# Two-layer trunk: the output projections begin with the rows that don't come from attention, keys and values stay on chip, the S5 output comes back in 8 loads, extra tiles accumulate over 4 row tiles

## The chip, the cores and the metric

The kernel runs on one core of a Trainium2 chip. The metric is device microseconds of one execution. The program before was run three times: 1918.76, 1931.55 and 1936.65 us, median 1931.55. A fourth number, of a profiled execution, belongs to the profile below.

## The reference, cut to what matters

Two layers over a sequence of 512 rows, width 2048, all in float32. Each layer modulates a normed input by a condition `c`, projects it, runs two mixers, gates each, and projects their concatenation back.

```python
def layer_attn_s5(x, c, ...):                       # layer 0
    h, gate = ada_modulate(x, c, norm_g, ada_w, ada_b)
    q, k, v, g_a, u, g_b = split_cols(h @ w_in, (1024, 256, 256, 1024, 1024, 1024))
    q, k = rope(rms_norm(q)), rope(rms_norm(k))
    o_a = gqa_block_attention(q, k, v) * jax.nn.silu(g_a)
    o_b = s5_mixer(u, ...) * jax.nn.silu(g_b)       # scan both ways, gelu, then y @ w_glu + b_glu, GLU
    return x + gate * (jnp.concatenate([o_a, o_b], axis=-1) @ w_out)

def layer_na_ssd(x, c, ...):                        # layer 1
    ...
    o_c = neighbourhood_attention(q, k, v, rpb) * jax.nn.silu(g_c)
    o_d = ssd_mixer(z, xbc, dt_raw, ...)
    return x + gate * (jnp.concatenate([o_c, o_d], axis=-1) @ w_out)
```

So rows 0 to 1023 of an output projection's input come from attention, rows 1024 to 2047 from S5 with its GLU (layer 0) or from SSD (layer 1). The S5 state passes work on 64 groups of 16 channels.

## The kernel before, in words

Every product of float32 matrices is made of three matmuls on values that are split into a high and a low part (`mm3`, L164 to L166, 512 columns each; `runit`, L228 to L230, 256 columns). Weights come in pieces of up to 128x1024 by `w_issue`, in the order of `plan0` and `plan1`, into two raw buffers; `w_prep` splits them (ACT copies the high part, L125, DVE subtracts for the low part, L126) into three buffers, and each unit takes the next (`w_take`). All DMAs are issued by one queue, SP's, in the order of the program.

The main line of the program is a list of units for TensorE: `tunit` (one output tile of 128 rows, 8 weight tiles of 128x128 to a weight piece), `runit` (the transposed kind, for q, k, v) and `out_units`. Beside it run generators ("streams"): after every few matmuls a unit calls `slot()`, which advances every stream by a step (by two while `sstep` is `SSLOT`). `finish(name)` calls slots until a stream ends. A scheduler orders the instructions of each engine by priorities; a slot's instructions have a higher one. PSUM has eight banks of 128x512: `m0` to `m3` and `b0` to `b3`. `mbank` turns through the first `nmain` of m0, m1, m2, m3. `tbank`, the bank for transposes, turns between `b2` and `m3` where `nmain` is under 4, and is always `b2` where it is 4.

Layer 0, in order:

- Input projection, k = 0 to 15: `ada_sum` (L966) sums the shift and scale of one row tile from two loaded buffers, `ada_cols` makes row tile k of `h`, and six banks accumulate 6 of the 8 tiles of `u`. Six further outputs (2 tiles of `u`, 4 gates of the S5 path) are the extra units: each takes a piece over 2 row tiles with 3 outputs, accumulates 6 matmuls in bank `b2`, and DVE adds the bank to `xacc` in SBUF (L1035; the first group is copied by ACT). They run at k = 2 to 17.
- The S5 stream (`s5_in`, `s5_scan`, `s5_kernels`, `s5_out`), which stores y to DRAM in 8 stores (L580). Beside it TensorE makes the gates `gb`, `ga` (`gate_evict`: L882 to L884, through `r2k`, a tile with a single buffer) and the k and v projections. `kv_evict` copies each bank by ACT to `r2k` (L1088), stores it to `kvd` (L1089), and both are loaded back (L1101) to G12 and G13.
- After the S5 stream: the rope tables (stream "tab"), `y_load` (L893: 64 loads of 16 partitions, 32 KB each, one for each group), and `ada_stream`, which reads 128x1024 pieces of the conditioning weights (L609), and reduces each with one DVE instruction (L623), one or two pieces to a slot by `ADAP`.
- Attention in four chunks (`gqa_stream`, 8 score steps to a chunk): scores, maximum (DVE, L828), exponent (ACT, L831), scaling (DVE, L837), four transposes into one bank (L813), a cast and a split (L125, L126), and the values. TensorE runs q projections and gates beside it, later the GLU units that read y (split on DVE at L1132).
- `finish("oa")`, the loads of the gated attention output, and then `out_units` from half 0, the attention's rows, with `nmain` 4.

In layer 1 the same `out_units` ran from half 1, after `finish("na")`.

Of the kernel before, what the change touches and what calls it, by code (L numbers as in the profile page):

```python
# [22 lines left out]
PRI_ADA = 3000  # L23
ADAP = "22221111"
NFIRST = 4
# [7 lines left out]
N1 = 6  # L33
AO = 6
S5K = (0, 0, 2, 2, 3, 3, 3, 4, 4, 4, 4, 4, 4, 3, 5, 5)
# [32 lines left out]
class Trunk:  # L68
# [111 lines left out]

    def out_units(self, rhs, evict, first, halves=False):

        bk = []
        for half in (first, 1 - first):
            for j in range(NFIRST):
                if half == first:
                    bk.append(self.mbank())
                wh, wl = self.w_take()
                for k8 in range(8):
                    c = slice(k8 * 128, k8 * 128 + 128)  # L190
                    self.mm3(bk[j], wh[:, c], wl[:, c], *rhs(half * 8 + k8), half == first and k8 == 0,
                             half != first and k8 == 7)
# [694 lines left out]
    def y_load(self, tag, ydram):  # L887

        ys = self.sl(tag, [128, 8, 8, 64])
        yv = ydram.rearrange("(t h) g c -> g h t c", h=16)  # L890
        for k in range(8):
            for g in range(8):
                self.nc.sync.dma_start(out=ys[16 * g:16 * g + 16, k], in_=yv[k * 8 + g])  # L893
            yield
        self.ys = lambda k: ys[:, k].rearrange("p t c -> p c t")
# [19 lines left out]
    def layer0(self):  # L915
        nc, A = self.nc, self.A
# [5 lines left out]
        def ada_load(k, qs=range(4)):  # L922
            if k < 16:
                if 0 in qs:
                    abuf[k] = big[k % 2].rearrange("p (q n) -> p q n", q=4)
                i = 2 * k - AO
# [92 lines left out]
        def extra(k):  # L1019

            wh, wl = self.w_take()
            g, half = k // 2 - 1, k % 2
            for i in range(3):
                e = 3 * half + i
                ps = self.bank("b2")
                for kk in range(2):
                    c = slice((3 * kk + i) * 128, (3 * kk + i) * 128 + 128)
                    self.mm3(ps, wh[:, c], wl[:, c], *self.h_rhs(2 * g + kk), kk == 0, kk == 1)
                if g == 0:
                    if e % 2 == 0:  # L1030
                        xacc.append(self.sl((G[16], G[17], G[0])[e // 2], [128, 2, 512]))
                    nc.scalar.copy(out=xacc[e // 2][:, e % 2], in_=ps)
                    continue
                t = xacc[e // 2][:, e % 2]
                nc.vector.tensor_tensor(out=t, in0=t, in1=ps, op=ALU.add)  # L1035
                if g == 7:
                    xev[e](t)

        for k in range(16):
# [10 lines left out]
            if k >= 2:  # L1050
                extra(k)
            for _ in range(S5K[k]):
# [13 lines left out]
        def s5_rest():  # L1066
            yield from self.s5_in([G[14], G[3], G[1], G[2], G[15], G[16], G[17]], st)
            a, b = self.s5_scan(st), self.s5_kernels(G[14:18])
            la = lb = True
            while la or lb:  # L1070
                la = la and next(a, "end") != "end"
                lb = lb and next(b, "end") != "end"
                yield
            yield from self.s5_out([G[14], G[15], G[3], G[16], G[10], G[17], G[11], G[0], G[2], G[1]], st, ydram)
        self.start("s5", s5_rest())
        self.sstep = SSLOT
        extra(17)
        for j in range(4, 8):
# [3 lines left out]
        kvd = self.scratch("kvd", [2, 128, 4, 256])  # L1082

        def kv_evict(i):
            def ev(bk):
                for j, b in enumerate(bk):
                    t = self.gt()
                    nc.scalar.copy(out=t, in_=b)  # L1088
                    nc.sync.dma_start(out=kvd[i][:, 2 * j:2 * j + 2].rearrange("p t c -> p (t c)"), in_=t)  # L1089
            return ev  # L1090
        for i in range(2):
            self.runit(self.h_lhs, (4, 4, 4, 4), 256, kv_evict(i))
        self.finish("s5")
        self.sstep = 1
        self.nmain = 4
        self.start("tab", self.qk_tables((G[8], G[10]), G[9]))
        self.start("yload", self.y_load("OLa", ydram))
        self.start("ada", self.ada_stream(range(3), G[15:18]))
        raw = [self.sl(t, [128, 4, 256]) for t in (G[12], G[13])]
        for i in range(2):  # L1100
            nc.sync.dma_start(out=raw[i], in_=kvd[i])  # L1101
        for j in GAK:
            self.tunit(self.h_rhs, 16, self.gate_evict(ga[j]))
        self.finish("tab")
        self.nmain = 3
        self.start("kT", self.gqa_k(raw[0], G))
        self.gqa_v(raw[1], G)
        aux = self.sl("OLb", [128, 4, 1024], F32R)
# [30 lines left out]
        for j in range(8):  # L1139
# [12 lines left out]
            for e in (ev_gate, ev_val):  # L1152
                self.tunit(lambda k: (yh(k), yl(k)), 8, e)
        self.finish("oa")
        self.nmain = 4
# [14 lines left out]
        def out_evict(j):  # L1170
# [22 lines left out]
            return ev  # L1193
        self.out_units(o_rhs, out_evict, 0, True)

# [454 lines left out]
    def layer1(self):  # L1650
# [125 lines left out]
        for c in range(4):  # L1776
            for nm, tg in (("k", G[14]), ("v", G[15]), ("q", G[16])):
# [22 lines left out]
        def out_evict(j):  # L1800
# [7 lines left out]
            return ev  # L1808
        self.out_units(o_rhs, out_evict, 1)

# [29 lines left out]
def host_layer0(I):  # L1840
# [17 lines left out]
    f["w0_u"] = w[:, 2560:3328].reshape(16, 128, 768)  # L1858
    f["w0_x"] = w[:, 3328:4096].reshape(8, 2, 128, 2, 384).transpose(0, 3, 2, 1, 4).reshape(8, 2, 128, 768)
# [3 lines left out]
    g = t_units(a("s5_w_glu")[0])  # L1863
    f["w0_glu"] = np.stack([g[8:], g[:8]], axis=1).reshape(16, 1, 128, 1024)
# [23 lines left out]
def plan0(A):  # L1888
    p = []
    for k in range(18):  # L1890
        if k < 16:
            p.append(A["w0_u"][k])
        if k >= 2:
            p.append(A["w0_x"][k // 2 - 1, k % 2])
# [6 lines left out]
    p += out_pieces(A["w0_out"], 0)  # L1901
    return p
# [74 lines left out]
```

## Time and profile before

| | before |
|---|---|
| median of 3 runs | 1931.55 us (1918.76 to 1936.65) |
| profiled execution | 1918.29 us, its span 1916.5 us |
| mean granted TensorE clock | 0.98 |
| PE / PEld / DVE / ACT busy in the span | 93% / 80% / 64% / 38% |
| DMA packets, bytes | 143243, 349.63 MB |

The profile gives the busy time of each engine over the span of one execution. PE is TensorE's matmul, PEld its weight load, DVE the VectorE, ACT the ScalarE, SP the engine that issues all DMAs. The rows of tenths cut the span into 40 slices of 47.9 us; a 9 is 90% or more, and in the clock's row 9 is the full granted clock. A wait names the instruction or DMA that ended the idle time of an engine. L12 is line 12 of the kernel.

### The profile page before, as it was taken

The page shows a single profiled execution, that of the slowest core. Times are in us where ns is not written, and L with a number is a line of the kernel's source. Part 1 is how long each engine was busy: PE and PEld are TensorE (multiplying, and loading weights), DVE is VectorE, ACT ScalarE, POOL GpSimd, SP SyncE. Part 2 cuts the span into 40 slices and gives each one's busy share as a digit, 9 for nine tenths or more (in the row PEclk, how much of TensorE's full clock was granted, in tenths as well). Part 3 has the DMA queues.
Part 4 walks back from the last instruction along what each step waited for, and adds up shares of the span by engine and source line. Part 5 has one row for each costly group of instructions (what it writes and reads, how often), then busy time and mean ns, then how long its engine had stood idle before and what let it go on. Part 6 is the DMA issues. An engine that isn't in the chain of part 4 may idle for free.

```text
span 1916.5 us, 28952 instructions
## 1 busy us (share of the span) xinstructions
PE 1791.1 (93%) x11176; PEld 1528.2 (80%) x11176; DVE 1230.5 (64%) x2357; ACT 731.5 (38%) x1360; POOL 38.7 (2%) x51
## 2 busy tenths in 40 slices
PE   5988799899949999979999999999999999999999
PEld 2755579689848987867888987887689999998887
DVE  7896667895558999963236567568986645544322
ACT  5432236325413544432224324435655434433211
POOL 2000000000000000001110000000000000000000
PEclk9999999999969999999999999999999999999999
DMA  8987452856789879745443573246743333342542
GB/s 316 355 308 263 114 138 76 267 162 207 235 271 318 297 240 307 242 138 165 140 140 102 175 265 102 88 123 204 217 144 128 104 105 98 101 141 76 191 143 88
DMA packets 143243, 349.63 MB, mean 182 GB/s; under 512 B 32544, under 2 KB 43712, under 8 KB 143104
## 3 DMA queue, kind: packets, MB, share of 16 engines
q1 hardware_dynamic: 143104, 347.77, 56.3%
q8 instruction: 88, 1.44, 0.3%
q14 instruction: 51, 0.42, 0.1%
HBM read 311.53 MB, written 34.61 MB: 181 GB/s over the span
## 4 chain that ended last, share of the span: by engine, by line
PE 56%; DVE 18%; DMA 17%; issue 4%; ACT 3%; SPq 1%; POOL 0%; DVEq 0%; ACTq 0%
PE m L164 11%; PE m L165 10%; PE m L166 10%; DMA G<-in_ada_r_dram 8%; PE m L228 5%; PE m L229 5%; PE m L230 5%; DVE wl L126 3%; DVE G L623 3%; DMA G<-s_ck 2%; PE b L164 2%; DVE w2k L477 2%; PE b L165 2%; DMA G<-csd 2%; PE b L166 1%
## 5 line engine op out<-in xcount | busy, mean ns | idle before, releaser
L125 ACT CAST wh<-w 128x1024 fp32r<-128x1024 f32 (+3 forms) x266 | 269.9, 1016 | 613.6 <-PE m L165 310.8
L126 DVE TENSOR_TENSOR wl<-w,wh 128x1024 fp32r<-128x1024 f32 (+3 forms) x266 | 314.9, 1184 | 276.5 <-ACT wh L125 267.9
L164 PE MATMUL m<-H,wh 128*128 128x512 f32 (+1 forms) x968 | 383.8, 400 | 4.9 <-ACT wh L125 3.5
L228 PE MATMUL m<-wh,H 128*128 128x256 f32 (+2 forms) x1232 | 355.4, 289 | 30.7 <-ACT r2k L1088 29.6
L165 PE MATMUL m<-H,wh 128*128 128x512 f32 (+1 forms) x968 | 382.3, 396 | 0.0
L166 PE MATMUL m<-H,wl 128*128 128x512 f32 (+1 forms) x968 | 378.2, 397 | 1.3 <-DVE wl L126 1.3
L230 PE MATMUL m<-wh,H 128*128 128x256 f32 (+2 forms) x1232 | 355.2, 290 | 0.0
L229 PE MATMUL m<-wl,H 128*128 128x256 f32 (+2 forms) x1232 | 354.3, 288 | 0.0
L228 PEld LDWEIGHTS m<-wh,H 128*128 128x128 f32 x1232 | 235.1, 191 | 35.7 <-ACT r2k L1088 30.2
L229 PEld LDWEIGHTS m<-wl,H 128*128 128x128 f32 x1232 | 235.1, 191 | 2.7 <-issue 1.0
L230 PEld LDWEIGHTS m<-wh,H 128*128 128x128 f32 x1232 | 234.5, 191 | 3.3 <-issue 1.7
L164 PEld LDWEIGHTS m<-H,wh 128*128 128x128 f32 x968 | 183.9, 190 | 51.3 <-ACT wh L125 7.3
L166 PEld LDWEIGHTS m<-H,wl 128*128 128x128 f32 x968 | 182.8, 189 | 43.6 <-issue 2.6
L165 PEld LDWEIGHTS m<-H,wh 128*128 128x128 f32 x968 | 183.3, 189 | 41.5 <-issue 3.7
L623 DVE SCALAR_TENSOR_TENSOR G<-G,cb 128x1024 f32<-128x1024 f32 x128 | 155.4, 1221 | 72.8 <-DMA G<-in_ada_r_dram 57.1
L164 PE MATMUL b<-H,wh 128*128 128x512 f32 x128 | 53.9, 430 | 11.8 <-DVE G L1035 11.6
L1388 ACT ACTIVATE G<-G,G 128x128 f32<-128x128 f32 x128 | 39.9, 390 | 49.8 <-DMA G<-csd 44.7
L1035 DVE TENSOR_TENSOR G<-G,b 128x512 f32<-128x512 f32 x42 | 28.6, 682 | 40.4 <-PE b L166 40.4
L164 PE MATMUL m<-OLb,wh 128*128 128x512 f32 (+1 forms) x132 | 50.1, 389 | 2.7 <-ACT OLb L125 2.7
L164 PE MATMUL m<-OLa,wh 128*128 128x512 f32 (+1 forms) x132 | 51.3, 391 | 0.2 <-ACT wh L125 0.2
L166 PE MATMUL m<-OLa,wl 128*128 128x512 f32 (+1 forms) x132 | 51.1, 387 | 0.0
L165 PE MATMUL b<-H,wh 128*128 128x512 f32 x128 | 51.1, 402 | 0.0
(395 smaller groups left out, 2754.7 us busy)
## 6 DMA issues: line engine op xcount, KB each, us to landing
G<-in_ada_r_dram SPq DMA_DIRECT2D x128, 512.0 KB
w<-in_w_kvq_dram SPq DMA_DIRECT2D x72, 512.0 KB
w<-in_w_out_dram SPq DMA_DIRECT2D x64, 512.0 KB
OLa<-in_ada_dram SPq DMA_DIRECT2D x32, 512.0 KB
OLb<-in_ada_dram SPq DMA_DIRECT2D x32, 512.0 KB
G<-s_ck SPq DMA_DIRECT2D x32, 512.0 KB
w<-in_w_x_dram SPq DMA_DIRECT2D x24, 512.0 KB
s_ck<-G SPq DMA_DIRECT2D x16, 512.0 KB
```

The source lines that it names most:

```text
L125: self.nc.scalar.copy(out=hi, in_=src)
L126: self.nc.vector.tensor_tensor(out=lo, in0=src, in1=hi.bitcast(F32), op=ALU.subtract)
L164: mm(out=out, lhsT=lh, rhs=rh, start=start, stop=False)
L165: mm(out=out, lhsT=lh, rhs=rl, start=False, stop=False)
L166: mm(out=out, lhsT=ll, rhs=rh, start=False, stop=stop)
L228: mm(out=o, lhsT=hi, rhs=wh[:, c], start=(k == 0 and i % per == 0), stop=False)
L229: mm(out=o, lhsT=hi, rhs=wl[:, c], start=False, stop=False)
L230: mm(out=o, lhsT=lo, rhs=wh[:, c], start=False, stop=last)
L477: tt(out=pt[..., g], in0=src, in1=self.s5_lt[..., g], op=ALU.mult)
L623: nc.vector.scalar_tensor_tensor(out=t, in0=t, scalar=1.0, in1=cb, op0=ALU.mult, op1=ALU.mult, accum_out=o)
L1035: nc.vector.tensor_tensor(out=t, in0=t, in1=ps, op=ALU.add)
L1388: nc.scalar.activation(out=r[:, d, c], in_=r[:, d, c], func=AF.Relu, scale=-1.0, bias=dv["hi"][:, c, 16 * d + h:16 * d + h + 1])
```

## The change

Five edits:

1. `out_units` always starts with half 1 for the first four output tiles (the S5/GLU or SSD rows), and calls `ready()` (the `finish` of the attention's output) before half 0. Layer 0's weight order follows. `nmain` is set to 4 before the rest of the attention's steps.
2. `raw_evict` copies k and v to G12 and G13, and the store and reload of `kvd` go. The rope tables move into the S5 stream, between `s5_in` and the scan. The k and v preparation starts before the gate units `GAK`, which now turn through 3 banks.
3. `y_load` is 8 loads of 128 partitions (256 KB); the host orders the rows of the GLU weights to match.
4. Extra units take 4 row tiles with 2 outputs: 12 units of 24 matmuls (12 per bank), at k = 4 to 18 but not where k % 4 is 3, instead of 16 units of 18.
5. `ADAP` from 22221111 to 22111111: the group 1 of the ada stream does one piece to a slot instead of two.

```diff
-ADAP = "22221111"
+ADAP = "22111111"
...
-    def out_units(self, rhs, evict, first, halves=False):
+    def out_units(self, rhs, evict, ready, halves=False):
         bk = []
+        first = 1
         for half in (first, 1 - first):
+            if half != first:
+                ready()
...
-        yv = ydram.rearrange("(t h) g c -> g h t c", h=16)
+        yv = ydram.rearrange("(t k h) g c -> k (h g) t c", t=8, k=8)
         for k in range(8):
-            for g in range(8):
-                self.nc.sync.dma_start(out=ys[16 * g:16 * g + 16, k], in_=yv[k * 8 + g])
+            self.nc.sync.dma_start(out=ys[:, k], in_=yv[k])
             yield
...
         def extra(k):
+            g, part = k // 4 - 1, k % 4
+            if g < 0 or part == 3:
+                return
             wh, wl = self.w_take()
-            g, half = k // 2 - 1, k % 2
-            for i in range(3):
-                e = 3 * half + i
-                ps = self.bank("b2")
-                for kk in range(2):
+            for i in range(2):
+                e = 2 * part + i
+                ps = self.bank("b3" if g == 3 and i else "b2")
+                for kk in range(4):
...
+            yield from self.qk_tables(("ropeq", "ropek"), G[8])
...
         for i in range(2):
-            self.runit(self.h_lhs, (4, 4, 4, 4), 256, kv_evict(i))
+            t, ev = self.raw_evict(G[12 + i])
+            kvraw.append(t)
+            self.runit(self.h_lhs, (4, 4, 4, 4), 256, ev)
         self.finish("s5")
         self.sstep = 1
-        self.nmain = 4
-        self.start("tab", self.qk_tables((G[8], G[10]), G[9]))
         self.start("yload", self.y_load("OLa", ydram))
         self.start("ada", self.ada_stream(range(3), G[15:18]))
-        raw = [self.sl(t, [128, 4, 256]) for t in (G[12], G[13])]
-        for i in range(2):
-            nc.sync.dma_start(out=raw[i], in_=kvd[i])
+        self.nmain = 3
+        self.start("kT", self.gqa_k(kvraw[0], G))
+        self.gqa_v(kvraw[1], G)
         for j in GAK:
             self.tunit(self.h_rhs, 16, self.gate_evict(ga[j]))
-        self.finish("tab")
-        self.nmain = 3
-        self.start("kT", self.gqa_k(raw[0], G))
-        self.gqa_v(raw[1], G)
...
-        self.finish("oa")
         self.nmain = 4
...
-        self.out_units(o_rhs, out_evict, 0, True)
+        self.out_units(o_rhs, out_evict, lambda: self.finish("oa"), True)
...
-        self.finish("na")
...
-        self.out_units(o_rhs, out_evict, 1)
+        self.out_units(o_rhs, out_evict, lambda: self.finish("na"))
```

SP's queue at the end of the S5 stage, before: the y loads (L893, of which these are the last), then gate loads, ada pieces, and the stores of k and v.

```order
L893 DMA OLa_626_4517<-ydram_1848 16x8x64 x6
L807 DMA G12_761_5461<-ga_252 128x512
L609 DMA G16_655_4719<-in_ada_r_dram 128x1024
L807 DMA G12_761_5461<-ga_252 128x512
L1089 DMA kvd_3560<-r2k_612_4407 128x512
L609 DMA G17_656_4722<-in_ada_r_dram 128x1024
L609 DMA G15_657_4745<-in_ada_r_dram 128x1024
L609 DMA G16_658_4748<-in_ada_r_dram 128x1024
L1089 DMA kvd_3560<-r2k_613_4410 128x512
```

The same queue in the change, from the last S5 store (L582) on; L894 is the y load, L138 a weight load, L886 the store of a gate.

```order
L582 DMA ydram_1735<-G2_584_4418 128x512
L611 DMA G16_600_4483<-in_ada_r_dram 128x1024
L138 DMA w_613_4558<-in_w0_kvq_dram 128x1024
L611 DMA G15_614_4574<-in_ada_r_dram 128x1024
L894 DMA OLa_591_4449<-ydram_1735 128x8x64 x4
L611 DMA G17_608_4545<-in_ada_r_dram 128x1024
L894 DMA OLa_591_4449<-ydram_1735 128x8x64 x2
L611 DMA G16_607_4542<-in_ada_r_dram 128x1024
L894 DMA OLa_591_4449<-ydram_1735 128x8x64 x2
L138 DMA w_620_4606<-in_w0_kvq_dram 128x1024
L886 DMA ga_252<-r2k_609_4549 128x512
```

No store of k and v stands in it any more, and the y loads all stand behind the last S5 store. On DVE, 58 ada pieces stood ahead of the first y split before, 48 stand there in the change; in both 104 stand ahead of the last score step's scaling.

PE near the end of layer 0's attention, before: two transposition groups (L813), one into `b2` and the next into `m3`, with value matmuls (`b3`) between them.

```order
L166 MATMUL b3_1077_7533<-OLb_662_4758,G3_661_4755 128x256
L813 MATMUL b2_1090_7618<-ident_4_76,G9_1063_7479 128x128 x4
L164 MATMUL b3_1092_7631<-G10_1086_7604,G2_660_4754 128x256
L813 MATMUL m3_1093_7644<-ident_4_76,G14_1064_7480 128x128 x4
L165 MATMUL b3_1092_7631<-G11_1087_7605,G2_660_4754 128x256
```

A few rows later the last group, and behind it the first matmuls of the output projection, which read the attention's output (`OLa`).

```order
L166 MATMUL b3_1092_7631<-G10_1086_7604,G3_661_4755 128x256
L813 MATMUL b2_1095_7657<-ident_4_76,G14_1064_7480 128x128 x4
L164 MATMUL m2_1114_7721<-OLa_1096_7678,wh_1057_7411 128x512
L164 MATMUL m0_1122_7783<-OLa_1096_7678,wh_1119_7753 128x512
```

PE in the change, some steps earlier: output tiles that read GLU rows (`H16` to `H31`) stand between the groups of transposes (L815).

```order
L164 MATMUL m0_1044_7416<-H31_874_6368,wh_1041_7386 128x512
L165 MATMUL m0_1044_7416<-H30_873_6367,wl_1042_7387 128x512
L815 MATMUL m3_986_7045<-ident_4_76,G14_943_6797 128x128 x4
L815 MATMUL b2_996_7105<-ident_4_76,G14_943_6797 128x128 x4
L163 MATMUL m1_1048_7447<-H16_859_6353,wh_1045_7417 128x512
L164 MATMUL m1_1048_7447<-H17_860_6354,wh_1045_7417 128x512
L163 MATMUL m2_1035_7333<-OLa_1085_7677,wh_1049_7448 128x512
```

And where the last eight groups begin, all of which go to `b2`, with matmuls of the output projection's half 0 beside a few of them.

```order
L165 MATMUL b1_1070_7562<-G0_625_4647,OLb_629_4658 128x512
L163 MATMUL m0_1044_7416<-OLa_1085_7677,wh_1095_7742 128x512
L164 MATMUL m0_1044_7416<-OLa_1085_7677,wh_1095_7742 128x512
L815 MATMUL b2_1064_7519<-ident_4_76,G9_1052_7466 128x128 x4
L165 MATMUL m0_1044_7416<-OLa_1085_7677,wl_1096_7743 128x512
```

The first four output tiles hold banks m0 to m3 from their half 1 until their half 0 is done. Twelve score steps stand behind the last GLU unit in both orders.

## Rows read from the trace of the kernel before

**Rows 1.** The page: the span, the busy time of each engine (share of the span) and its instructions, and three of the rows of 40 slices.

```profile
span 1916.5 us, 28952 instructions
PE 1791.1 (93%) x11176; PEld 1528.2 (80%) x11176; DVE 1230.5 (64%) x2357; ACT 731.5 (38%) x1360; POOL 38.7 (2%) x51
PE   5988799899949999979999999999999999999999
DVE  7896667895558999963236567568986645544322
PEclk9999999999969999999999999999999999999999
```

**Rows 2.** Busy time by stretch of the span: from:to and length in us, busy us of PE, PEld, DVE, ACT and POOL with the instructions in brackets, then the granted clock, the DMA share and GB/s.

```profile
46.00:200.00 154.00, 136.89 (x912) 94.55 (x904) 127.06 (x223) 51.38 (x74) 0.43 (x2) 0.98 0.81 293
200.00:240.00 40.00, 32.21 (x134) 23.29 (x135) 22.61 (x34) 9.40 (x14) 0.00 (x0) 0.96 0.56 126
525.00:556.00 31.00, 1.44 (x7) 1.25 (x7) 12.21 (x19) 2.67 (x3) 0.00 (x0) 0.57 0.90 264
550.00:560.00 10.00, 5.25 (x25) 5.25 (x26) 3.70 (x6) 1.02 (x2) 0.00 (x0) 0.51 0.92 308
556.00:800.00 244.00, 238.91 (x1485) 214.49 (x1485) 219.51 (x427) 102.59 (x205) 0.14 (x2) 0.98 0.85 286
800.00:857.00 57.00, 45.58 (x253) 36.43 (x252) 44.60 (x101) 25.75 (x52) 0.14 (x2) 0.97 0.49 157
857.00:1020.00 163.00, 162.78 (x724) 132.70 (x723) 48.63 (x46) 42.50 (x48) 23.40 (x14) 1.00 0.47 147
900.00:920.00 20.00, 20.00 (x88) 16.24 (x87) 5.18 (x5) 4.40 (x6) 3.33 (x2) 1.00 0.47 145
1755.00:1775.00 20.00, 17.46 (x105) 14.56 (x103) 8.12 (x15) 5.74 (x11) 0.00 (x0) 1.00 0.14 41
```

**Rows 3.** The waits of the whole span that name the copies of k and v: who waited, for what; us in all, times, and the longest. The last row is ACT's timeline: start, duration, and in brackets the idle time before and what ended it.

```profile
PEld m L228 <- ACT r2k L1088: 30.2, 2, 30.0
PE m L228 <- ACT r2k L1088: 29.6, 1, 29.6
ACT r2k L1088 <- DMA kvd<-r2k: 22.1, 2, 19.0
554.11 0.59 ACT L1088 COPY r2k<-m 128x512 f32<-128x512 f32 x1 [18.98 <-DMA kvd<-r2k]
```

**Rows 4.** SP's queue in order of time, 480 to 660 us: start, time that the issues took, line, DMA, count.

```profile
491.64 1.82 SPq L893 DMA_DIRECT2D OLa<-ydram  x2
...
501.49 5.66 SPq L893 DMA_DIRECT2D OLa<-ydram  x10
...
543.73 2.80 SPq L893 DMA_DIRECT2D OLa<-ydram  x6
...
548.92 0.43 SPq L1089 DMA_DIRECT2D kvd<-r2k  x1
...
554.72 0.33 SPq L1089 DMA_DIRECT2D kvd<-r2k  x1
```

**Rows 5.** All instructions of a line: the y loads, the S5 stores, the y splits; shortest, median and longest in ns, then the first and last start in us.

```profile
L893 SPq DMA_DIRECT2D OLa<-ydram x64: 303/430/1138, 491.6 to 546.1; - x64
...
L580 SPq DMA_DIRECT2D ydram<-G x8: 321/378/585, 460.1 to 522.2; - x8
...
L1132 DVE TENSOR_TENSOR H<-OLa,H x8: 1080/1094/1115, 670.5 to 685.2; 128x512 fp32r<-128x512 f32 x8
```

**Rows 6.** Groups by line between 525 and 556 us: the ada pieces on DVE; busy us, mean ns, then the idle time before them and what ended it.

```profile
L623 DVE SCALAR_TENSOR_TENSOR G<-G,cb 128x1024 f32<-128x1024 f32 x9 | 11.0, 1224 | 15.1 <-DMA G<-in_ada_r_dram 15.1
```

**Rows 7.** The same view between 800 and 857 us, the end of layer 0's attention: maximum, ada pieces, transposes by bank, cast and split.

```profile
L828 DVE TENSOR_REDUCE sst<-b 128x1 f32<-128x512 f32 x12 | 8.2, 683 | 0.1
L623 DVE SCALAR_TENSOR_TENSOR G<-G,cb 128x1024 f32<-128x1024 f32 x8 | 9.8, 1222 | 4.5 <-DMA G<-in_ada_r_dram 4.4
L813 PE MATMUL b<-ident,G 128*128 128x128 f32 x32 | 4.9, 276 | 4.6 <-DVE G L837 4.6
L813 PE MATMUL m<-ident,G 128*128 128x128 f32 x28 | 4.8, 300 | 2.7 <-DVE G L837 2.5
L125 ACT CAST OLb<-b 128x512 fp32r<-128x512 f32 x4 | 2.3, 586 | 2.7 <-PE b L813 2.7
L126 DVE TENSOR_TENSOR OLb<-b,OLb 128x512 fp32r<-128x512 f32 x4 | 2.7, 682 | 0.0
```

**Rows 8.** The additions of the extra units (page), who waited for them (us, times), and, from 46 to 240 us, the matmuls of `ada_sum`.

```profile
L1035 DVE TENSOR_TENSOR G<-G,b 128x512 f32<-128x512 f32 x42 | 28.6, 682 | 40.4 <-PE b L166 40.4
...
  PE b L164: 11.6, 9
...
L966 PE MATMUL b<-OLb,cs 128*32 128x256 f32 x224 | 16.3, 420 | 3.5 <-DMA OLb<-in_ada_dram 1.9 <-issue 1.1 <-PE b L973 0.5
L966 PE MATMUL b<-OLa,cs 128*32 128x256 f32 x224 | 15.0, 385 | 6.2 <-DMA OLa<-in_ada_dram 5.8 <-DVE acols L982 0.5
```

More of the change, by code (lines that the diff above doesn't have):

```diff
@@ L33 @@
 N1 = 6
-AO = 6
 S5K = (0, 0, 2, 2, 3, 3, 3, 4, 4, 4, 4, 4, 4, 3, 5, 5)
@@ L925, in ada_load @@
                     abuf[k] = big[k % 2].rearrange("p (q n) -> p q n", q=4)
-                i = 2 * k - AO
+                i = k - 2 + 3 * max(0, (k - 6) // 4) + (min((k - 6) % 4, 3) if k > 6 else 0)
                 with self.tc.issue_after(self.wd[i].ins) if i in self.wd else nullcontext():
@@ L1019, in extra @@
         def extra(k):
+            g, part = k // 4 - 1, k % 4
+            if g < 0 or part == 3:
+                return
             wh, wl = self.w_take()
-            g, half = k // 2 - 1, k % 2
-            for i in range(3):
-                e = 3 * half + i
-                ps = self.bank("b2")
-                for kk in range(2):
-                    c = slice((3 * kk + i) * 128, (3 * kk + i) * 128 + 128)
-                    self.mm3(ps, wh[:, c], wl[:, c], *self.h_rhs(2 * g + kk), kk == 0, kk == 1)
+            for i in range(2):
+                e = 2 * part + i
+                ps = self.bank("b3" if g == 3 and i else "b2")
+                for kk in range(4):
+                    c = slice((2 * kk + i) * 128, (2 * kk + i) * 128 + 128)
+                    self.mm3(ps, wh[:, c], wl[:, c], *self.h_rhs(4 * g + kk), kk == 0, kk == 3)
                 if g == 0:
-                    if e % 2 == 0:
-                        xacc.append(self.sl((G[16], G[17], G[0])[e // 2], [128, 2, 512]))
-                    nc.scalar.copy(out=xacc[e // 2][:, e % 2], in_=ps)
+                    if i == 0:
+                        xacc.append(self.sl((G[16], G[17], G[0])[part], [128, 2, 512]))
+                    nc.scalar.copy(out=xacc[part][:, i], in_=ps)
                     continue
-                t = xacc[e // 2][:, e % 2]
+                t = xacc[part][:, i]
                 nc.vector.tensor_tensor(out=t, in0=t, in1=ps, op=ALU.add)
-                if g == 7:
+                if g == 3:
                     xev[e](t)
@@ L1049, in layer0 @@
                         first(ada_cols, k + 1)
-            if k >= 2:
-                extra(k)
+            extra(k)
             for _ in range(S5K[k]):
@@ L1077, in layer0 @@
         extra(17)
+        extra(18)
         for j in range(4, 8):
@@ L1081, in layer0 @@
             self.tunit(self.h_rhs, 16, self.gate_evict(ga[j]))
[L1082 to L1090, printed above, removed]
+        kvraw = []
         for i in range(2):
-            self.runit(self.h_lhs, (4, 4, 4, 4), 256, kv_evict(i))
+            t, ev = self.raw_evict(G[12 + i])
+            kvraw.append(t)
+            self.runit(self.h_lhs, (4, 4, 4, 4), 256, ev)
         self.finish("s5")
         self.sstep = 1
-        self.nmain = 4
-        self.start("tab", self.qk_tables((G[8], G[10]), G[9]))
         self.start("yload", self.y_load("OLa", ydram))
         self.start("ada", self.ada_stream(range(3), G[15:18]))
-        raw = [self.sl(t, [128, 4, 256]) for t in (G[12], G[13])]
-        for i in range(2):
-            nc.sync.dma_start(out=raw[i], in_=kvd[i])
+        self.nmain = 3
+        self.start("kT", self.gqa_k(kvraw[0], G))
+        self.gqa_v(kvraw[1], G)
         for j in GAK:
             self.tunit(self.h_rhs, 16, self.gate_evict(ga[j]))
-        self.finish("tab")
-        self.nmain = 3
-        self.start("kT", self.gqa_k(raw[0], G))
-        self.gqa_v(raw[1], G)
         aux = self.sl("OLb", [128, 4, 1024], F32R)
@@ L1858, in host_layer0 @@
     f["w0_u"] = w[:, 2560:3328].reshape(16, 128, 768)
-    f["w0_x"] = w[:, 3328:4096].reshape(8, 2, 128, 2, 384).transpose(0, 3, 2, 1, 4).reshape(8, 2, 128, 768)
+    f["w0_x"] = w[:, 3328:4096].reshape(4, 4, 128, 3, 256).transpose(0, 3, 2, 1, 4).reshape(4, 3, 128, 1024)
     f["w0_gb"] = t_units(w[:, 4096:4608])
@@ L1862, in host_layer0 @@
     f["w0_kvq"] = r_units(np.concatenate([w[:, 1024:1536], w[:, 0:1024]], axis=1))
-    g = t_units(a("s5_w_glu")[0])
+    g = t_units(a("s5_w_glu")[0].reshape(64, 16, 2048).transpose(1, 0, 2).reshape(1024, 2048))
     f["w0_glu"] = np.stack([g[8:], g[:8]], axis=1).reshape(16, 1, 128, 1024)
@@ L1889, in plan0 @@
     p = []
-    for k in range(18):
+    for k in range(19):
         if k < 16:
             p.append(A["w0_u"][k])
-        if k >= 2:
-            p.append(A["w0_x"][k // 2 - 1, k % 2])
+        if k >= 4 and k % 4 < 3:
+            p.append(A["w0_x"][k // 4 - 1, k % 4])
     seq = [("w0_gb", range(4)), ("w0_ga", GA0), ("w0_kvq", (0, 1)), ("w0_ga", GAK)]
@@ L1900, in plan0 @@
         p += [t[i, j] for i in js for j in range(t.shape[1])]
-    p += out_pieces(A["w0_out"], 0)
+    p += out_pieces(A["w0_out"], 1)
     return p
```

## The prediction

> **What bounds the kernel now.** I read the page's summary first, then a table of stages, then the waits, and last the lines of the stages that the change touches. The summary [rows 1] shows a program that is bound by TensorE: PE is busy 93% of 1916.5 us, and its row of tenths is 9 nearly throughout, with dips at slices 0 to 4, 7, 11 and 17. DVE is at 64% on the mean, but its tenths are 8 and 9 in the first 800 us. The table of stages [rows 2] sizes the dips. Between 525 and 556 us PE is busy 1.44 of 31 us; between 46 and 200 us it is idle 17.1 us, in the next 40 us 7.8, between 800 and 857 us 11.4, near the end of the program (1755 to 1775) 2.5. Elsewhere it is full: between 857 and 1020 us idle 0.2 of 163. So a time can only be won in those dips, and a step that adds work to DVE before 857 us is not free: in the stage of 556 to 800 us DVE is busy 219.5 of 244 us and the DMA engines 85%.
>
> The waits [rows 3] name the large dip: PE waits 30 us, once, for the ACT copy of L1088 into `r2k`, and that copy waits 19.0 us for the store `kvd<-r2k`, since `r2k` has one buffer. Why is the store late? SP's queue in order of time [rows 4]: the y loads of L893 stand in it from 491.64 us, one after another as the S5 stores that they need land, until 546.53; the `kvd` store behind them goes out at 548.92, the next at 554.72, when the copy behind it is made. One queue, two stores and one buffer stop PE.
>
> **Keys and values on chip, 8 y loads.** The copies now go to G12 and G13, which nothing stores, so the copy waits for no DMA: the PE idle time of 29.6 us goes (−29.6). The stall also leaves PE slow: between 550 and 560 us it is granted 0.51 of its clock and is busy 5.25 us, which would be 2.7 at the full of its two levels. I take −2.0. The y loads are covered either way: 64 issues of about 0.43 us, 27.5 us of SP, become 8; each needs the last S5 store (522.2 us) and the first reader, L1132, comes at 670.5 [rows 5], so they cost nothing; without that cover the cost would be the landing of 2 MB. Behind them on SP now stand a weight load and a gate store (the order of SP in the change); three split weight tiles, each 24 matmuls of 0.227 us (20 us for 88, 900 to 920 us, [rows 2]), cover 16 us, and the y loads wait about as long as one store. The rope tables move into the S5 stage, where they add no work.
>
> What is late next? DVE did 12.21 us of work inside the stall, 9 pieces of the ada stream in the main [rows 6]; that must now be done beside running matmuls. Behind 556 us DVE has 24.5 us idle, and the order of DVE in the change has 48 ada pieces ahead of the first y split where 58 stood (58 − 48 = 10, by 1.22 us, 12.2 us less DVE work there). So between a give-back of 0 and one of 12.2 I take +5, nearer to nothing, since the moved pieces just make room for the work.
>
> **Output projection from the other half.** After the last GLU unit twelve score steps are left in both orders (the order of PE). Before, nothing runs beside them: 57 us with 11.4 idle, 4.75 us per step. Now four half units, 4 × 24 × 0.227 = 22 us, can run before the attention is done. By the order they stand among the first of these steps; behind the last of them eight transposition groups are left, with only a few matmuls of the other half beside them. So a third of the idle time is covered, 3.8 of 11.4; those few (about 12 × 0.227 = 2.7) fill some of the rest: −6, between −11.4 and the loss in rival C. Price of the moved ada pieces here: 12.2 us of DVE between y split and the last step, where DVE has 12.4 idle from 800 us on. At the end of layer 1 the same edit can fill at most 2.5 idle us: −1, bounds −2.5 and 0.
>
> **Extra tiles over four rows.** The matmuls stay 288; the additions into `xacc` (L1035) go from 42 to 18, 24 × 0.68 = 16.4 us less on DVE. PE waits for them 11.6 us in all [rows 8]; 24 of 42 would be 6.6. Against it 72 matmuls, not 36, follow row 15: 36 × 0.227 = 8.2 us later, where PE is idle 7.8 us between 200 and 240: +0.4. I take −6. Best case is all idle time from 46 to 240 us, −24.9; worst +8.2. That the rest isn't DVE's shows in the waits of `ada_sum` (L966) for its loads, 5.8 and 1.9 us [rows 8], which the change leaves as they are.
>
> **Sum** against the profiled execution (1918.29 us): −29.6 − 2.0 + 5 − 6 − 1 − 6 = −39.6, 1878.7. That run lies 13.3 us under the median of the three runs; I add half of it, 6.6, for where a median will fall: **1885 us**.
>
> **Rivals.**
> A, the DMA engines are the next bound. Between 525 and 556 us they are busy 0.90 of the time, 27.9 us of work, mostly pieces that run ahead while PE stands. The two stages hold 31 × 264 GB/s + 244 × 286 GB/s = 78.0 MB; without `kvd` (1.5 MB there) 76.5, and in the 248 us that the forecast leaves (275 − 26.6) that is 308 GB/s: the rate of the busiest 10 us in [rows 2]. Only if the ten moved pieces (5.2 MB) leave the stage is it 287, as now. If they don't, the 27.9 us come back: −31.6 + 27.9 = −3.7 in place of −26.6, sum −16.7, 1901.6, with 6.6 **1908**. For it speaks the share of 0.85; against it that the waits of DVE for ada pieces don't hold PE.
> B, the first 240 us gain more: DVE is busy 127.06 of 154 us there, and 16.4 us less may loosen the whole chain of rows. With −20 for −6 the sum is −53.6: 1864.7, with 6.6 **1871**. Against it speak the DMA waits named above.
> C, slower: the last chunk's transposition groups, eight of them, now all use bank `b2`, where before `b2` and `m3` took turns (`nmain` becomes 4 earlier; the orders of PE show it). If that sets the steps end to end, each costs the sum of its parts [rows 2, 7]: PE 45.58/12 = 3.8, DVE without ada (44.60 − 9.8)/12 = 2.9, 11 ada pieces over 8 steps 1.7, ACT 25.75/12 = 2.1: 10.5 us where a step takes 4.75. Eight times the difference is 46; 46 − 4 = +42 in place of −6, sum +8.4, 1926.7, with 6.6 **1933**. It decides from (33.6 + 4)/8 + 4.75 = 9.45 us per step. Against it: a group holds its bank for four transposes (4 × 0.28), the cast 0.59 and the split 0.68, 2.4 us [rows 7], half a step; and where the transposes wait, it is for the scaling L837 (4.6 and 2.7 us, nearly all), never for a bank.
> The Trainium skill ("Perfetto Trace Analysis", section Matmul Optimizations) asks that all eight PSUM banks be in use, to keep as many instructions as possible in flight; by that rule taking one away costs, and the sum would be that of C. No row above bears it out for this stage.
>
> **Numbers.** The forecast has 0.71 (its own range is 1866 to 1900), A 0.15, B 0.09, C 0.05. The range for 8 in 10 takes in B and A and leaves out C and what lies past A: the best of all terms (−29.6 − 2.6 − 11.4 − 2.5 − 24.9 = −71.0, 1854 with 6.6) bounds it below, so **1852 to 1916**. About 1%, 19 us, is what a measurement of this kernel can tell from no change. Faster by more (under 1912): the forecast nearly whole, B, and over half of A: 0.86. Within 1%: the rest of A, a little of the forecast, and most of C: 0.11. Slower: 0.03, C with steps still longer.
>
> **What would show it.** In the changed profile: PE busy around the end of S5, no wait for a copy into a single buffer, 8 y loads after the last S5 store. DVE in the stage after it near 90% and PE near 98%; if PE waits there for weights' splits and the DMA share is over 0.9, it was A. 18 additions, and PE's wait for them near 5 us; if PE's idle time from 46 to 240 us is under 10, it was B. In the attention's tail PE idle near 5 us; transposes that wait for a split or a cast of the same bank, and steps over 9 us, are C. Wrong altogether would be an idle gap of PE of over 10 us in a place where there is none now, above all behind the y loads on SP's queue.

## The result, and the profile after

The changed kernel takes 1848.32 us (median of 4 runs, 1847.69 to 1849.15); the kernel before 1925.15 (4 runs), ratio 0.961, interval 0.953 to 0.968. That is faster by more than the forecast's best case: 1848 lies under the range of 1852 to 1916. The runs of the changed kernel lie within 1.5 us, those of before within 27.

The changed kernel's page answers to [rows 1], and a table of stages to [rows 2]:

```profile
span 1846.8 us, 28836 instructions
PE 1778.2 (96%) x11176; PEld 1523.9 (83%) x11176; DVE 1212.2 (66%) x2329; ACT 728.5 (39%) x1356; POOL 38.9 (2%) x51
PE   5999999899999999889999999998999999999999
DVE  6697697994689999842256575577985453644332
PEclk9999999999999999999999999999999999999999
```

```profile
46.00:200.00 154.00, 148.65 (x972) 106.15 (x973) 126.14 (x217) 56.30 (x79) 0.42 (x2) 0.99 0.83 309
200.00:240.00 40.00, 39.60 (x204) 33.12 (x202) 22.61 (x32) 16.69 (x22) 0.00 (x0) 1.00 0.76 188
480.00:720.00 240.00, 239.71 (x1508) 216.05 (x1507) 215.81 (x412) 104.13 (x205) 0.00 (x0) 1.00 0.89 301
720.00:812.00 92.00, 79.52 (x402) 63.84 (x400) 69.37 (x146) 33.03 (x62) 0.27 (x4) 0.98 0.57 187
1680.00:1720.00 40.00, 37.43 (x179) 30.88 (x178) 16.58 (x25) 10.02 (x18) 0.00 (x0) 0.91 0.38 128
```

The account adds up: PE's idle time over the span falls from 1916.5 − 1791.1 = 125.4 to 1846.8 − 1778.2 = 68.6 us (−56.8), and the same 11176 matmuls are busy 12.9 us less; together −69.7, the difference of the spans. Some 8 of the 12.9 us are the clock: busy time by the missing share of the clock, summed over slices of 10 us, is 20.6 us before and 12.6 now. What the other 5 us are is not shown. By stage: from 46 to 240 us PE was idle 24.9 us and is now idle 5.8 (−19.1); the gap of 29.6 at the k and v copies is gone; the rest of the attention (556 to 857 before, 480 to 812 now) goes from 16.5 to 12.8. The gap left no trace behind it: from 480 to 720 us PE is idle 0.3 us. At the end of layer 1 nothing was won: the stretch that was idle 2.8 us before (below) is idle 2.6 us now, and its clock is 0.91.

```profile
1750.00:1790.00 40.00, 37.25 (x191) 30.63 (x190) 18.41 (x29) 10.35 (x19) 0.00 (x0) 1.00 0.42 130
```

The additions of the extra units after, for [rows 8]: their line, what they waited for, and who waited for them; and `ada_sum` (now L967) between 46 and 240 us.

```profile
L1038 DVE TENSOR_TENSOR G<-G,b x18: 679/687/699, 133.4 to 235.0; 128x512 f32<-128x512 f32 x18
  PE b L165: 10.2, 8
  PEld b L163: 2.4, 3
  PE b L163: 1.5, 3
```

```profile
L967 PE MATMUL b<-OLa,cs 128*32 128x256 f32 x224 | 15.6, 418 | 1.4 <-PE b L974 1.4
L967 PE MATMUL b<-OLb,cs 128*32 128x256 f32 x224 | 14.8, 385 | 0.0
```

PE waits 1.5 us for additions instead of 11.6, and the ada loads, of which the prediction said that the change leaves their waits as they are (7.7 us), no longer hold PE here at all.

### The profile page after: what moved, and what is told of

The parts are those of the page before. It is cut to its first block, busy times and chain, and to the rows that moved or that the text cites. A ratio compares the mean times of both kernels' runs of the same rounds, so it can differ in the third digit from the quotient of the medians.

```text
span 1846.8 us, 28836 instructions
## 1 busy us (share of the span) xinstructions
PE 1778.2 (96%) x11176; PEld 1523.9 (83%) x11176; DVE 1212.2 (66%) x2329; ACT 728.5 (39%) x1356; POOL 38.9 (2%) x51
## 5 line engine op out<-in xcount | busy, mean ns | idle before, releaser
L125 DVE TENSOR_TENSOR wl<-w,wh 128x1024 fp32r<-128x1024 f32 (+2 forms) x262 | 314.5, 1201 | 269.3 <-ACT wh L124 266.9
L124 ACT CAST wh<-w 128x1024 fp32r<-128x1024 f32 (+2 forms) x262 | 269.2, 1029 | 555.4 <-PE m L164 283.3
L163 PE MATMUL m<-OLb,wh 128*128 128x512 f32 (+1 forms) x132 | 50.8, 395 | 2.7 <-ACT OLb L124 2.7
L165 PE MATMUL m<-OLb,wl 128*128 128x512 f32 (+1 forms) x132 | 52.4, 397 | 0.0
L163 PE MATMUL b<-H,wh 128*128 128x512 f32 x128 | 50.9, 405 | 1.5 <-DVE G L1038 1.5
L164 PE MATMUL m<-OLb,wh 128*128 128x512 f32 (+1 forms) x132 | 52.2, 396 | 0.0
```

Of the source, the lines that this page charges most:

```text
L124: self.nc.scalar.copy(out=hi, in_=src)
L125: self.nc.vector.tensor_tensor(out=lo, in0=src, in1=hi.bitcast(F32), op=ALU.subtract)
L163: mm(out=out, lhsT=lh, rhs=rh, start=start, stop=False)
L164: mm(out=out, lhsT=lh, rhs=rl, start=False, stop=False)
L165: mm(out=out, lhsT=ll, rhs=rh, start=False, stop=stop)
```

## The experiments

In the tables of this section "lost" is PE's time lost between matmuls: from one start to the next, what is over the usual distance of the same pair of matmuls, summed over a stage of the profiled run. It holds idle time and time at the lower clock. For the kernel before it is 213 us in all (91 before 280 us of the span, 35 from 420 to 580, 27 from 700 to 880), for the changed one 144 (58, 2, 21). It depends on what is taken as usual: with the median of the pair the sums come out up to 5 us apart (11 to 14 in all), so a difference of 2 or 3 us in these columns says little. It is that of one execution, where "us" is the median of several. The kernel before took 1924 to 1927 us beside e1 to e12 and 1917 to 1919 beside e13 to e17, where the changed kernel was not run again: against its 1848.3 the times of those five can stand some 7 us too low.

**Each part alone, on the kernel before** (1924 us beside these runs). The edits are the hunks of the diff above.

> The kernel before with the extra tiles over 4 row tiles alone (their weight pieces and the issue of the ada loads with them). Theory 1 (the missed 28 us lie in the input projection, and this edit alone brings them): PE's lost time from 0 to 280 us falls by about 34 us, the gap of 30 us at the k and v copies stays, 1925 - 34 = about 1891 us. Rival (the forecast's term was right, and the rest came from the parts acting together): 1919 us, and the wait of PE for the ada loads stays.

> The kernel before with keys and values kept on chip alone (rope tables in the S5 stream, banks of the gate units with it). Theory 1: the stall of 30 us goes whole, with nothing given back: 1925 - 32 = 1893 us. Rival (DMA or DVE give back part in the stage behind): 1900 to 1910 us, with PE waits for split weights or ada pieces between 556 and 800 us.

> The kernel before with the output projections from half 1 alone. Theory 1: -5 us, 1920 us, with PE's lost time around the last score steps about 14 us for 18. Rival (one transposition bank for the last chunk costs): PE waits for a bank or a split in the last eight steps take what the half units gain: 1925 to 1935 us.

> The kernel before with the 8 y loads alone. Theory 1 (the store of k and v is late because 64 y loads stand ahead of it on the queue, each waiting for an S5 store): with 8 loads behind the last S5 store the first kvd store goes out earlier or at the same time, the stall shortens by at most the issue time of the y loads, so between 1900 and 1925 us. Rival (the y loads are not the reason, r2k's one buffer is): no change, 1925 us, with a gap as long as before.

| part alone | us | ratio (interval) | lost before 280 / 420 to 580 / 700 to 880 |
|---|---|---|---|
| extra tiles over 4 rows | 1888.6 | 0.984 (0.978 to 0.990) | 58 / 34 / 18 |
| k and v on chip | 1912.5 | 0.996 (0.993 to 0.998) | 88 / 14 / 33 |
| half 1 first | 1918.0 | 0.997 (0.995 to 0.999) | 92 / 33 / 18 |
| 8 y loads | 1906.9 | 0.991 (0.988 to 0.994) | 95 / 9 / 32 |

The extra tiles bring what theory 1 said. For k and v alone it missed: the gap at the copies goes, but a gate's copy, which still uses `r2k`, then stops PE, and the last score steps lose 6 us more; of the 30 us 11 come out. The view is that of waits in that kernel:

```profile
PE m L164 <- DVE r2k L883: 8.4, 1, 8.4
```

The 8 loads alone take the same gap away, though k and v still go through DRAM: at the place of the old gap PE is full, and on SP's queue (second fence) the `kvd` stores stand ahead of the y loads.

```profile
525.00:556.00 31.00, 31.00 (x229) 29.47 (x228) 18.06 (x26) 6.87 (x12) 0.00 (x0) 1.00 1.05 318
```

```profile
507.00 0.32 SPq L1088 DMA_DIRECT2D kvd<-r2k  x1
...
511.83 0.33 SPq L1088 DMA_DIRECT2D kvd<-r2k  x1
...
526.31 5.86 SPq L892 DMA_DIRECT2D OLa<-ydram  x4
```

So the cause of the stall was the queue: 64 loads, each reading what an S5 store wrote, in front of a store that one buffer waited for. How much of their 55 us on the queue is waiting for those stores, and how much the 27.5 us of their own issues, these runs don't separate: 30 of the 64 were issued behind the last S5 store (522.2 us). And each removal of the gap alone gives some of it back in the last score steps (32 to 33 us lost for 27).

**One part undone, on the changed kernel** (1848.3 us).

```diff
# e5: out_units as before, finish("oa") ahead of it, weights from half 0
# e6: kv_evict with kvd, and the reload before gqa_k; tables and banks as changed
# e7: y_load with 64 loads
# e8: ADAP = "22221111"
```

> The changed kernel (1848 us) with its output projections as before (layer 0 from half 0, attention finished first). Theory 2 (without the stall the attention's last steps stand bare: they lost 27 to 31 us of PE in the kernels with only the y loads or only k and v changed, for 17.5 before, and the half units cover that): PE loses about 30 us in the last score steps for 21 in the changed kernel, 1858 to 1866 us. Rival (the reorder is worth what it brought alone, 6 us): 1852 to 1855 us.

> The changed kernel with k and v stored to DRAM through r2k and loaded back, as before; rope tables and banks stay as changed. Theory 2 (the 64 y loads on SP's queue made the store late; with 8 loads behind the last S5 store it isn't): no gap at the copies, at most the reload's wait, 1848 to 1856 us. Rival (one buffer is enough to stop PE): a gap of 20 us or more, 1870 to 1880 us.

> The changed kernel with the 64 y loads of 32 KB as before. Theory 2 (any store behind the y loads on the queue is late, so the gate units, which still go through r2k, wait as they did for 8.5 us in the kernel with only k and v changed): 1854 to 1862 us, PE idle 8 us or more behind the copy or the gate of r2k. Rival (nothing behind the loads matters once k and v stay on chip): 1848 us.

> The changed kernel with ADAP 22221111 as before: the ada stream's second group two pieces to a slot. Theory 2 (DVE and DMA have room in that stage: the changed kernel shows no PE loss from 540 to 720 us): 1848 us within 4. Rival A of the prediction (the stage is at the limit of DVE or DMA, and the moved pieces make the room): PE waits for split weights between 500 and 720 us, 1856 to 1870 us.

| undone | us (range) | lost 420 to 580 / 700 to 880 |
|---|---|---|
| half 1 first | 1860.2 (1859.6 to 1864.1) | 3 / 32 |
| k and v on chip | 1857.9 (1856.4 to 1859.7) | 1 / 28 |
| 8 y loads | 1862.3 (1857.0 to 1866.5) | 13 / 26 |
| ADAP | 1855.2 (1852.6 to 1857.8) | 1 / 27 |

The expectation of e5 held; e6 and e7 came out in the manner of theory 2, 2 and 0.3 us over its bounds. The half units are worth 12 us here, twice their worth alone, and most of it lies in the last score steps. k and v on chip are worth 10 us although their trip through DRAM leaves no gap: that, too, is lost in the last steps, so theory 2 was low by a few us there. The y loads stop a gate instead of k and v. ADAP missed both expectations: 7 us, but no wait for split weights; the loss lies in the last steps (27 for 21), and why earlier pieces make those lose more was not tried. All these parts lose time in one place, the last score steps, beside what they lose where they stand.

**What in the extra units.** Theory 3: an addition that stands in DVE's line and waits for PE holds up the splits and row tiles behind it, and these the ada loads. The waits from 46 to 280 us speak for it (waiter, what it waited for; us, times, longest), before and after:

```profile
DVE G L1035 <- PE b L166: 39.6, 19, 5.9
SPq L139 <- DVE wl L126: 91.1, 26, 7.9
```

```profile
DVE G L1038 <- PE b L165: 10.2, 8, 2.1
SPq L138 <- DVE wl L125: 60.6, 21, 15.2
```

```diff
# e9: two accumulations to a unit's output
+                for r in range(2):
+                    ps = self.bank("b3" if g == 3 and i else "b2")
+                    for kk in range(2 * r, 2 * r + 2):
...
# e10: in SBUF, one or two times behind each addition, 24 in all
+                    nc.vector.tensor_tensor(out=t, in0=t, in1=t, op=ALU.max)
# e11: extra units as before, but
-                nc.vector.tensor_tensor(out=t, in0=t, in1=ps, op=ALU.add)
+                nc.scalar.copy(out=w, in_=ps)
+                nc.gpsimd.tensor_tensor(out=t, in0=t, in1=w, op=ALU.add)
# e12
-NFIRST = 4
+NFIRST = 3          # and nmain = 4 only after finish("oa")
```

> The changed kernel with the same pieces over 4 row tiles at the same places, but each output summed in two accumulations of 2 row tiles: 6 matmuls to a bank and 42 additions, as before. Theory 3 (it is the additions that stand in DVE's line and wait there for PE: 39.6 us of DVE before, 10.2 in the changed kernel, and behind them wait the splits of weights, behind those SP and the ada loads): most of the 34 us come back, 1868 to 1882 us, PE waits for the additions and the ada loads again. Rival (the pieces' size, place and bytes do it): 1848 to 1854 us.

> The changed kernel with 24 more DVE instructions in the extra units, a maximum of the sum in SBUF with itself (the same value), 24 x 0.68 = 16 us of DVE, none of which waits for PE. Theory 3: at most a third of the 16 us shows, 1848 to 1854 us. Rival (DVE's busy time itself sets the input projection, the forecast's rival B): 1860 to 1866 us.

> The changed kernel with the extra units as before (16 units of 2 row tiles, 6 matmuls to a bank), but ACT copies each bank to SBUF and POOL adds, so that no addition stands in DVE's line. Theory 3: most of the gain stays, 1850 to 1860 us, and PE waits for ACT's copy of the bank instead of the addition by a few us. Rival (short sums in one bank stop PE whoever empties it): 1870 to 1882 us.

> The changed kernel with three output tiles open instead of four, so that m3 stays for the transposes of layer 0's last chunk, which take turns in b2 and m3 to the end (layer 1 has three open tiles, too). Rival C of the prediction (one bank holds the steps up): PE loses less in the last score steps than the 21 us of the changed kernel, 1840 to 1845 us. Theory 2 (the last steps wait for DVE and ACT, and only cover helps): a quarter of the cover goes, 5.5 us, of which a half shows, 1849 to 1854 us.

| kernel | us (range) | lost before 280 |
|---|---|---|
| e9, sums of 6 matmuls | 1888.7 (1887.3 to 1893.1) | 86 |
| e10, 24 more on DVE | 1853.1 (1848.4 to 1864.9) | 60 |
| e11, old units, ACT empties the bank | 1894.7 (1892.0 to 1898.4) | 88 |
| e12, three open tiles, two banks | 1850.6 (1846.4 to 1851.2) | 58 |

e9 is the clear one: the same pieces, loads and places, and only the length of a sum changes; 40 us. In its waits (46 to 300 us) the additions are back:

```profile
DVE G L1039 <- PE b L165: 28.5, 18, 5.7
PE b L163 <- DVE G L1039: 11.4, 9, 3.9
```

The last link of theory 3 is not. From 46 to 280 us SP waits 80.1 us for split weights (60.6 in the changed kernel), but no ada load holds `ada_sum` between 46 and 240 us (first fence, e9); it waits for DVE's reading of its bank. With the old extra units (e14 below, second fence) the loads hold it again, 6.0 us.

```profile
L967 PE MATMUL b<-OLb,cs 128*32 128x256 f32 x224 | 16.3, 403 | 4.2 <-DVE acols L983 4.2
L967 PE MATMUL b<-OLa,cs 128*32 128x256 f32 x216 | 13.3, 382 | 0.5 <-PE b L974 0.5
```

```profile
L967 PE MATMUL b<-OLb,cs 128*32 128x256 f32 x224 | 15.2, 389 | 2.8 <-DMA OLb<-in_ada_dram 2.2 <-PE b L974 0.5
L967 PE MATMUL b<-OLa,cs 128*32 128x256 f32 x211 | 14.4, 390 | 3.8 <-DMA OLa<-in_ada_dram 3.8
```

Between the two stands a line that the list of the change does not name: with the fourth edit each ada load is issued behind another weight piece (`i` in `ada_load`). e9 keeps the new place, e14 and e11 have the old one, and in e11, where no addition stands on DVE, the view names no ada load either. So the loads hold PE only where the old place and the additions on DVE come together, and e9 shows that the 40 us don't hang on them.

e10 speaks against DVE's busy time as the cause (+5 us for 16 us of work, 2 of it in the input projection). Its profiled execution is the slowest of the four, 1864.9 us, for a stretch at the lower clock behind the input projection (last section). e11 came out on the rival's side, above its bounds, but it moved the line instead of removing it: now ACT, which also casts the weights and makes the row tiles, stands waiting for PE, and then for POOL's slower addition (1.56 us in the median, for 0.68 on DVE). The lines are those of its copy (L1038), what its idle time waited for.

```profile
  PE b L165: 42.2, 24
  POOL G L1039: 14.7, 4
```

e12 gave the transposes their second bank back; 1850.6 against 1848.3 is no gain. It also left one half unit less beside the last steps, which its expectation priced at some 3 us, so a price of the single bank of that size is not excluded; one of the size of rival C (+42 us) is.

**The line, or PE's order alone?**

```diff
# e13: after the matmuls of j = 2 and 5, for k = 2 to 13; e17: after every j, at a higher priority
+                    nc.vector.tensor_copy(out=wl[:, j * 128:j * 128 + 1], in_=self.ones)
# e15: 8 row tiles and one output to an extra unit, 12 units, 6 of them behind row 15
# e16: ADAP = "11111111"
```

> The changed kernel with 24 tiny DVE instructions (one column of a weight tile's low part, overwritten after its last reader on PE, so it changes no result), two for each row tile from 2 to 13, each of which must wait for PE. No hand-over of a bank is added. Theory 3 (what waits for PE in DVE's line holds up what stands behind it): 10 to 25 us slower than 1848, DVE idle behind them as long as behind the additions of before (some 30 us). Rival (the hand-overs of the one bank stop PE; who waits is of no account): 1846 to 1853 us.

> The changed kernel with the extra units as before. Both theories: the 34 us of the first experiment come back, 1880 to 1890 us. If it is 1865 us or less, the parts of the change overlap.

> The changed kernel with extra units over 8 row tiles, one output each: 24 matmuls to a bank, 6 additions, 12 hand-overs; half of the units (144 matmuls) come behind row 15, and the first stands at row 8. Theory 3 and its rival: a few us from fewer waits (PE waits 1.9 us for the additions in the changed kernel), but the early rows lose the matmuls that fill PE while a row tile is made: between 1843 and 1865 us. PE's idle time before 120 us tells how much filling is worth.

> The changed kernel with ADAP 11111111, one ada piece to a slot from the start. If pieces that come later relieve the stage (7 us for 16 pieces in e8): 1842 to 1846 us. If they now fall beside the last score steps: 1850 to 1860 us, with more than 21 us lost there.

> The changed kernel with 72 tiny DVE instructions (six for each row tile from 2 to 13, 72 x 0.15 = 11 us of DVE) that wait for PE and are placed early in DVE's line; no hand-over of a bank is added, and no result changes. If DVE now stands idle behind them 20 us or more: theory 3 says 1862 to 1880 us, with PE waiting for splits and row tiles; the rival says 1850 to 1856 us. If it stands idle under 10 us again, the run says nothing and the question stays open.

| kernel | us (range) | lost before 280 |
|---|---|---|
| e13, 24 waits on DVE | 1852.6 (1848.4 to 1857.8) | 59 |
| e14, old extra units | 1902.1 (1892.7 to 1910.2) | 92 |
| e15, 8 row tiles | 1875.2 (1865.1 to 1881.4) | 65 |
| e16, one ada piece to a slot | 1852.9 (1852.3 to 1856.3) | 58 |
| e17, 72 waits on DVE | 1849.7 (1845.1 to 1853.8) | 59 |

e13 and e17 answer nothing: where the scheduler put these instructions, PE had mostly been done, and DVE stood idle before them 5.9 and 5.3 us (the lines of e17, what its idle time waited for).

```profile
  PE m L165: 4.5, 6
  PE b L165: 0.8, 2
```

So it stays open how much of the 28 us that e9 loses before 280 us is the emptier's line and how much is PE's own order, in which everything behind a hand-over is late. e15 shows the other end: with sums over 8 rows the whole kernel is 27 us slower, above its bounds. PE is idle 4.7 us from 46 to 120 us (2.1 in the changed kernel), where it has less to fill the time in which a row tile is made, and 6.4 from 120 to 280 us (3.6); that is a third of the 17 us that the profiled execution loses, itself the fastest of the four by 9 us. The rest is not explained. e16 gives nothing. In e14 the old extra units cost 54 us, 19 more than on the kernel before and above the bounds of both theories; its profiled execution, 8 us over the median, loses 18 us more from 420 to 580 us than the changed kernel, in a stretch at the lower clock (last section).

No variant was clearly faster than the changed kernel.

## Why the prediction was right and wrong

- **Keys and values, y loads: −29.6 right, give-back wrong in place.** The gap went whole, and the stage behind it runs at 99.9% with a DMA share of 0.89 and 301 GB/s. So the +5 was not paid there. It is paid in the last score steps, by e2 and e4 with some 6 us, and there the half units cover it. The prediction called the y loads "covered either way" and priced them at nothing; e4 shows that they alone hold the stall. The profile had it in [rows 4], and the prediction read it there as the cause, but then took only the loads' issue time as the price of the edit. Since k and v on chip take the same gap away, the sum didn't suffer.
- **Clock: −2.0 was too little.** Over the whole program the clock costs 8 us less (20.6 to 12.6), and the matmuls are 12.9 us shorter. The gap at 525 us was one place; before, the clock also fell in the input projection behind waits (0.93 from 100 to 150 us, where it is now 1.0). A wait that goes takes its clock loss with it, and the term counted one place only.
- **Output projections: −6; 12 in the changed kernel, 6 alone.** Mechanism and place right. The size depends on what else is late there: without the gap the last steps lose more (32 to 33 us for 27 in e2 and e4). So the sign, PE idle near 5 us in the tail, did not come: it is idle 12.5 us from 720 to 812 us. At the end of layer 1 the term of −1 is not borne out (2.8 us idle before, 2.6 now).
- **Extra tiles: −6, the step that failed.** It took 24 of 42 of the direct waits of PE for the additions, and held that the rest is not DVE's, since `ada_sum` waits for its loads and the change leaves these as they are. The waits for the loads went, and the edit does not leave them: it moves their issue, too. But they are not what was won: with the sums short again PE waits directly 11.4 us for the additions and not for the loads, and 40 us are lost (e9). The length of a sum is worth several times its direct waits. Idle time from 46 to 240 us fell by 19.1 us of the 24.9 that the prediction gave as its best case; alone, the edit is worth 35 us by the medians, 30 by the ratio. A row that hints at it was shown: [rows 8], 40.4 us in which DVE stood idle before L1035 with PE as the reason. The prediction read that line for who waits for the addition, and not for what stands behind it on DVE. Whether it is DVE's line or PE's own order that carries the rest stays open (e13, e17).
- **Rivals.** B came true, in the size of its term (−20) and its sign in the profile (PE idle under 10 us from 46 to 240 us), though not for its reason, DVE's busy time, against which e10 speaks. It was told as a case beside the forecast, with the stall's terms unchanged and 5 of give-back. By stage the difference of spans is −29.6 (the gap) − 19.1 (46 to 240 us) − 3.7 (the rest of the attention) − 4.4 (idle time elsewhere) − 12.9 (shorter matmuls) = −69.7. A fell (share 0.89, PE full). C fell: from 700 to 880 us the transposes of the changed kernel wait 0.9 us for a split, and e12 gains nothing.

The range reached down to 1852, since it started from the profiled run and added 6.6 for the median; the changed kernel's median lies at its own profiled run, and what varied before, by 27 us, no longer does.

The Trainium skill ("Perfetto Trace Analysis", section Optimizing Tensor Performance, Matmuls) asks that independent accumulations rotate through banks, so that emptying one overlaps the next. The trace agrees with the point of the rule: sums that take turns in one bank cost 40 us when they are half as long (e9); in the input projection all eight banks are taken, so none was left to rotate to. The Trainium skill's rule that all eight banks be in use (same page, section Matmul Optimizations), which the prediction named for rival C, shows no gain for the transposes (e12, with one half unit less beside them).

## What to carry to other kernels

Where an accumulator has one bank, try longer sums, as long as the operands that are there allow: halving the hand-overs was worth 35 us here. Halving them again cost 27, in part because the early rows then have less to fill PE. When an instruction waits for PE, look at the idle time before it as well as at who waits for it: what stands behind it in its engine's line may be held up, too; here that reading fits e9 and was not shown by itself. On a queue that issues in order, loads that depend on earlier stores stood in the way of every store behind them; look for the buffers that those hold. And ask whether the execution that a trace shows is like the median: those of e10 and e14 were not.

## What the runs showed of the hardware

In two of the 19 profiled executions, e14 and e10, PE is busy without a break for some 37 us, and yet its clock is granted near the lower of its two levels for all that time. The rows are e14 (two), e10, and the changed kernel:

```profile
420.00:450.00 30.00, 29.19 (x244) 28.82 (x242) 27.53 (x87) 7.89 (x10) 0.00 (x0) 1.00 0.29 86
450.00:490.00 40.00, 40.00 (x201) 40.00 (x199) 6.66 (x10) 15.90 (x26) 0.00 (x0) 0.53 0.49 159
412.00:449.00 37.00, 37.00 (x176) 37.00 (x175) 5.99 (x10) 13.95 (x23) 0.00 (x0) 0.50 0.51 161
414.00:454.00 40.00, 40.00 (x358) 40.00 (x357) 17.38 (x37) 27.17 (x57) 0.00 (x0) 1.00 0.82 261
```

174 of the 201 matmuls of e14 are those of the S5 output, with 64 columns. But these narrow matmuls are not the reason: the changed kernel runs the same stage, 300 of its 358 matmuls of the same two lines, with narrow and wide in the same order, and at the full clock. One of them takes 0.27 us there for 0.40 in e14 (first line, 450 to 490 us; the second is the changed kernel, 414 to 454 us).

```profile
L569 PE MATMUL b<-G,G 128*128 128x64 f32 x116 | 28.1, 395 | 0.8 <-ACT G L556 0.8
L569 PE MATMUL b<-G,G 128*128 128x64 f32 x200 | 29.6, 273 | 0.0
```

So a stretch in which PE never stands idle can still be granted half of the clock, here for some 18 us of loss, in one execution and not in another with the same matmuls. In both kernels the execution that shows it is the slowest of those measured (1910.2 us for a median of 1902.1; 1864.9 for 1853.1). What decides it stays open; just before it PE waited once, 0.8 us in e14 and 0.7 in e10, for ACT (L556), but it did so, 0.6 us, in the kernel before, too, and kept the full clock.
